# Softmax numerators copied SBUF to SBUF into a float32r buffer and transposed there, in a four-layer forward pass on one core

## The chip, the core and the metric

One core of a Trainium2 chip runs the whole program. The metric is the device time of one execution in microseconds, the median of several runs. Every array is float32. "float32r" is the type that the kernel uses for its fast matrix products: float32 bytes, rounded when an engine writes them.

## The reference, cut to what matters

Two blocks that mix a gated spatial product with grouped-query attention, then a gated-linear-attention layer, then a convolutional feed-forward layer, 1024 tokens of width 1024. The change is in the attention of the first two blocks (`D_B` 512, 8 query heads of 64 features, 2 key/value heads):

```python
def attend(qblk):
    sc = jnp.einsum('bqkgd,bskd->bkgqs', qblk, k).astype(jnp.float32) * scale
    p = jax.nn.softmax(sc, axis=-1).astype(v.dtype)
    return jnp.einsum('bkgqs,bskd->bqkgd', p, v)
```

After it, `x = x + rmsnorm(concat(y_a, y_b) @ w_out) * post_g`, where `y_a` comes from the spatial half.

## The kernel before, in words

Every float32 product runs as three float32r products over an exact split of each factor into a rounded part (hi) and the rest (lo). `split` (L71) makes a pair: ACT or DVE copies to float32r, DVE subtracts.

The order of TensorE's instructions is that of the program text (`manual_schedule`, L79). The orders on DVE, ACT, POOL and SP are made by a planner with its own estimates of time, before the run. All loads and stores but seven go through SP (`load`, L68), which serves its queue in order: an instruction that waits holds what is queued behind it. The planner puts a load into that queue where it expects its buffer to be free.

The attention of a layer goes by 16 groups (g), a group being 128 query tokens and one key/value head, that is 4 heads. A group has 8 units (u). In the unit (g, u):

- `turn(g, u)` (L479) transposes on PE four blocks of 128 x 128 of the softmax numerators P: two heads, two key tiles. The block is the stationary operand and a float32 identity is streamed through it (L490). ACT and DVE then split the result from PSUM into one of 8 buffers PT (`XA`, L491 to 493). The PSUM tile "tr" has two buffers, and a third one is borrowed in part of the first two groups.
- `scores(g + 1)` (L453) does half of one head's scores for the next group; with every second unit a head is complete, DVE takes its row maximum (L467), and ACT writes exp(S - max) as float32 into one of 7 buffers (`XB`, L468 and 470). The heads are made in the order 0, 2, 1, 3. Heads 0 and 2 are transposed in units 0 to 3 of the next group, heads 1 and 3 in units 4 to 7.
- `attend` (L505) multiplies V with the PT of three units before.
- one step of the output projection `project` of an earlier token tile (L533), three products of 512 columns; the first starts at unit 2 of group 2.
- in unit 1 the next queries are transposed, four blocks of 128 x 128 in float32r with the float32r identity `identr` (`prep_turn`, L405); in unit 2 a small gate (L501); in unit 7 of every second group a tile of `y_a` (`turn_ya`, L528, transposes in L147).

In the last group (g = 15), at u = 1, 2, 3, the first three token tiles of the next norm are fetched and normalised in buffers 1, 2, 3 of `XB`, with buffer 3 or 4 as a place for squares that nobody reads (L600 to 602). `XB[:, 7]` holds `qf` and `ya`, the landing places of the queries' and `y_a`'s loads.

Two slots of 32 KiB (`big`, L105) hold the transposed activations h^T in the projections, then PT and P, and at the end the last gate and sums.

Of the kernel before, what the change touches and what calls it, by code (L numbers as in the profile page):

```python
# [36 lines left out]
def build(tc, a):  # L37
    """The whole forward pass on one core.

    Float32 products run as three float32r passes over an exact split x = hi + lo  # L40
    (hi = x rounded to float32r, lo = x - hi): hi*hi + hi*lo + lo*hi.
    """
# [47 lines left out]
    def rstd_of(ss, n=1):  # L90
        """(ss + EPS) ** -0.5"""
        v = T(cst, [128, n], f"ve{n}", bufs=4)
        nc.vector.tensor_scalar(out=v, in0=ss, scalar1=EPS, scalar2=None, op0=ALU.add)  # L93
        r = T(cst, [128, n], f"rs{n}", bufs=4)
        tt(r, v, nhalf[:, 0:n], ALU.pow, nc.gpsimd)
        return r
# [8 lines left out]
    def big(i, dt=F32R):  # L105
        """One of the two 32 KiB slots that hold h^T, the attention's P^T and P, the last gate and sums."""
        return T(xpool, [128, 8192], f"X{i}", dt)

    def hT_half(i):
        return big(i).rearrange("p (s k t) -> p s k t", s=2, k=KT)  # L110

    class Weights:
        """Streams chunks [128, 1024] of packed weights into exact hi/lo pairs, in two pools of 3 and 5 buffers;
        the chunks of the second last for one projection only."""
# [27 lines left out]
    def to_T(src, dst, c0, ps_pool, n, k0=0, tag="tr"):  # L142
        """dst[:, hi/lo, k0 + k, c0:c0 + 128] = src[:, 128 k:128 (k + 1)]^T, k < n."""
        for j in range(0, n, 4):
            ps = T(ps_pool, [128, 4, 128], tag, bufs=2 if tag == "tr" else 1)
            for k in range(4):
                nc.tensor.transpose(ps[:, k], src[:, (j + k) * 128:(j + k + 1) * 128], ident)  # L147
            split(dst[:, 0, k0 + j:k0 + j + 4, c0:c0 + 128],
                  dst[:, 1, k0 + j:k0 + j + 4, c0:c0 + 128], ps, on_act=True)

    def norm_scale(xt, xn, g, junk=None):
        """xn = rmsnorm(xt) * g"""
        ss = T(cst, [128, 1], "ss", bufs=4)
        act(xn if junk is None else junk, xt, AF.Square, scale=1.0 / 32, accum_out=ss)
        r = rstd_of(ss)
        stt(xn, xt, r, g, ALU.mult, ALU.mult)
# [7 lines left out]
    def mm3(ps, L, R, n):  # L164
        """ps = sum over k < n of L(k)^T R(k); L(k, s), R(k, s) give the hi (0) and lo (1) parts."""
        steps3(ps, L, R, range(n), 0, n - 1)

    def stat(hT, t):
        h, c = hT[t // 4], (t % 4) * 128
        return lambda k, s: h[:, s, k, c:c + 128]  # L170
# [9 lines left out]
    class Norms:  # L180
        """The token tiles of one norm, two ahead of their transposes into h^T."""
# [19 lines left out]
        def turn(self, j, tag="tr"):  # L201
            if self.at % 4 == 0 and j == 0:
                self.hT.append(hT_half(self.at // 4))
            t = self.at
            to_T(self.ready[t][:, 512 * j:], self.hT[t // 4], (t % 4) * 128, self.ps, 4, 4 * j, tag)
            self.at += j
# [10 lines left out]
    # ------------------------------------------------------------------ the first two layers  # L217
# [8 lines left out]
    for l in range(2):  # L226
# [11 lines left out]
        # A: norm, projections, gated spatial mixing  # L238
# [107 lines left out]
        def rope(dst, sq, qn, ps, n, i, t):  # L346
            """dst = rope(rmsnorm(ps) * g) of n heads of 64 for token tile t; sq and qn are for its use."""
# [27 lines left out]
        def turn_k(t):  # L375
            """K^T of the two heads, each in both halves of the partitions."""
            kd = kds.pop(t)
            pk = tr(F32R)[:, 0:2]
            for s in range(2):
                nc.tensor.transpose(pk[:, s], kd[:, s], identr)  # L380
            for v in range(2):
                for e in range(2):
                    nc.scalar.copy(Kst[64 * e:64 * e + 64, :, v, t * 128:t * 128 + 128], pk[64 * v:64 * v + 64])
# [27 lines left out]
        def gate_b(u, ps, th):  # L411
            """silu(g_b)^T * 2, a block of 128 features by 512 tokens; 4 steps."""
            hf, j = 1 - u // 4, u % 4
            for k in range(0, KT, 2):
                steps3(ps, wcols(ws[j:j + 1], 128), lambda k, s: hT[hf][:, s, k, :], range(k, k + 2), 0, KT - 1)
                if k < KT - 2:
                    yield
# [13 lines left out]
        # B: attention and, one token tile behind, the output projection  # L431
# [6 lines left out]
        XB = big(1, F32).rearrange("p (u k) -> p u k", u=8)  # L438
        qf, ya = XB[:, 7, 0:512], XB[:, 7, 512:1024]
# [13 lines left out]
        def scores(g):  # L453
            """Group g = (token tile, kv head): S, its maximum, exp; 8 steps."""
# [3 lines left out]
            for hh in (0, 2, 1, 3):  # L458
# [9 lines left out]
                P[hh] = XB[:, count[1] % 7]  # L468
                count[1] += 1
                act(P[hh], ps, AF.Exp, bias=nm, accum_out=sm[:, hh:hh + 1])  # L470
# [8 lines left out]
        def turn(g, u):  # L479
            """P^T of two heads for two key tiles, split; the gate over the row sums first."""  # L480
# [4 lines left out]
            ptr = T(psL, [128, 4, 128], "o" if third else "tr", bufs=1 if third else 2)  # L485
            ptr = ptr.rearrange("p (k e) t -> p k e t", k=2)
            for k in range(2):
                for e in range(2):
                    kt = 2 * k2 + k
                    nc.tensor.transpose(ptr[:, k, e], P[pr + 2 * e][:, kt * 128:kt * 128 + 128], ident)  # L490
            PT = XA[:, count[0] % 8]  # L491
            count[0] += 1
            split(PT[:, 0], PT[:, 1], ptr, on_act=True)
# [39 lines left out]
        def project(qt):  # L533
            """x_new(t) = x(t) + rmsnorm(y(t) w_out) * g_post; 16 steps."""
# [27 lines left out]
        XA = big(0).rearrange("p (u s k h t) -> p u s k h t", u=8, s=2, k=2, h=2)  # L562
# [4 lines left out]
        def step(*ks):  # L567
            """The next step of the oldest projection, if it is one of these, once for each unit (g, u)."""
# [7 lines left out]
        for g in range(2 * NT):  # L576
# [6 lines left out]
            for u in range(8):  # L583
# [15 lines left out]
                if g == 2 * NT - 1 and u in NU:  # L599
                    i = NU.index(u) + 1  # L600
                    norms.fetch(XB[:, i])
                    norms.start(XB[:, i], XB[:, 3 if i < 3 else 4])
# [14 lines left out]
    # ------------------------------------------------------------------ gated linear attention  # L617
# [27 lines left out]
    def f3(ps, L, R, start=True, stop=True):  # L645
        """ps (+)= L^T R of hi/lo pairs."""
# [12 lines left out]
    def split_alpha():  # L659
        """The low-rank weights: pairs of 16 columns [hi lo]; the rows of the second matrix are hi, the bias's hi  # L660
        and lo, hi and lo, against the rows hi, 1, lo and hi of the low-rank activations."""
# [11 lines left out]
    def alpha_low():  # L673
        for hf in range(2):
            ps = gmm()
            for k in range(KT):
                for s in range(2):
                    mm(ps, was[:, k], hT[hf][:, s, k, :], k == 0 and s == 0, k == KT - 1 and s == 1)
# [6 lines left out]
    def decays(h):  # L685
        """With b the running sum of log_sigmoid(...) / 16 over each tile of 128, less its value halfway:
        exp(b), exp(-b) and the decay from the middle of a tile to the middle of the next."""
# [24 lines left out]
    def chunks(h, v, rs, kT, sT, qq, gd):  # L712
        """The chunks of head h and their gated norm; two steps each."""
# [30 lines left out]
    for h in range(4):  # L744
# [4 lines left out]
        def of(x):  # L749
            """The hi and lo parts of tile t of a pair."""  # L750
# [20 lines left out]
        # k and q: feature-major, with their decays  # L771
# [3 lines left out]
        for hf in range(2):  # L775
            ps = gmm().rearrange("p (t i) -> p t i", t=4)
            mm3(ps.rearrange("p t i -> p (t i)"), wcols(ws, 128), lambda k, s: hT[hf][:, s, k, :], KT)
# [21 lines left out]
        for hf in range(2):  # L799
            ps = gmm().rearrange("p (t i) -> p t i", t=4)  # L800
            mm3(ps.rearrange("p t i -> p (t i)"), wcols(ws, 128), lambda k, s: hT[hf][:, s, k, :], KT)
# [11 lines left out]
        # silu(r), token-major, with the scores and, two tiles behind, the chunks  # L813
# [25 lines left out]
    # its output projection, and the next norm  # L839
# [6 lines left out]
    def turn_y(t):  # L846
        """y(t)^T; two steps."""
# [6 lines left out]
    def turn_x(t):  # L854
        """The norm of x_new(t) and its transpose; two steps."""
        xn = T(pH, [128, 1024], "xn", bufs=3)
        norm_scale(xts.pop(t), xn, g_pre)
        for j in (0, 4):
            to_T(xn[:, 128 * j:], hT[t // 4], (t % 4) * 128, psH, 4, j)
# [30 lines left out]
    # ------------------------------------------------------------------ convolutional FFN  # L890
# [12 lines left out]
    def up_mm(ps, w, hf):  # L903
        mm3(ps[:, 512 * hf:512 * hf + 512], w, lambda k, s: hT[hf][:, s, k, :], KT)
# [14 lines left out]
    def gsplit(n):  # L919
        gT = gX[:, n % 4]  # L920
# [4 lines left out]
    for hf in range(2):  # L925
        for n, (w, ps) in enumerate(first):
            up_mm(ps, w, hf)
            if hf == 0 and n == 1:
                to_T(xn, hT[1], 384, psU, KT)
            if hf == 1:  # L930
                up_use(n, ps)
    for n in range(3, 2 * FT):
# [3 lines left out]
        if n == 2 * FT - 1:  # L936
            gX = big(0).rearrange("p (u s k) -> p u s k", u=4, s=2)
# [8 lines left out]
    acc = big(1, F32).rearrange("p (t c) -> p t c", t=NT)  # L946
    load(acc, x_cur.rearrange("(t p) c -> p t c", p=128))
# [13 lines left out]
    def finish(t):  # L961
        """Two steps: the first half of the columns has its gain already."""
        act(acc[:, t, 0:512], acc[:, t, 0:512], AF.Identity, scale=rs[t])
        yield
        stt(acc[:, t, 512:], acc[:, t, 512:], rs[t], gf[:, 512:], ALU.mult, ALU.mult)
        load(tok(a["out"], t), acc[:, t])
        yield

    for c in range(2):
# [18 lines left out]
        for i, t in enumerate(order):  # L988
# [4 lines left out]
            sl = acc[:, t, 512 * c:512 * c + 512]  # L993
# [33 lines left out]
def _cols(w, n):  # L1027
    """[1024 or more rows, c] -> chunks [128, 1024]: for each block of n columns, groups of 1024 // n row tiles."""
# [56 lines left out]
```

## Time and profile before

| | |
|---|---|
| median of 3 runs | 2269.79 us (2268.68 to 2269.9) |
| span of the profiled execution, first to last instruction | 2268.4 us |
| granted TensorE clock, mean | 0.998 |
| busy: PE, DVE, ACT | 99%, 63%, 33% of the span |
| chain of work that ended last | PE 92%, DVE 3%, ACT 2% |
| attention of layer 0, first transposition to the last of its group 15 | 274.3 to about 541.3 us |
| attention of layer 1, the same | 824.1 to about 1091 us |

Of the profiled execution the profile gives the span alone. It lies 1.4 us under the median of the runs; what stands around it is not traced. The profile counts matmuls with their pipeline time, so "PE 99%" says that PE had work nearly always, not that it ran at its peak. What a change is worth is read from starts that follow each other.

### The profile page before, as it was taken

Reading aid. Unit: us, or ns where it says so; the run is one execution under the profiler, and the core shown is the slowest. Engines: PE = TensorE matmul, PEld = TensorE weight load, DVE = VectorE, ACT = ScalarE, POOL = GpSimd, SP = SyncE. Lnnn points to the kernel's source line nnn. Section 1 sums busy time; section 2 is a strip of 40 time slices with the busy share of each in tenths; the row PEclk is TensorE's granted clock in tenths of the full one; section 3 lists DMA queues with packets and bytes.
Section 4 is the critical chain, followed back from the end, with each engine's and each line's share of the span. In section 5 each row is a group of like instructions: output and inputs, shape, how many; then the busy total and the mean of one; then the engine's idle time right before and its main releaser. Section 6 shows DMA issues by size and latency. Waiting matters only on the chain.

```text
span 2268.4 us, 30078 instructions
## 1 busy us (share of the span) xinstructions
PE 2239.4 (99%) x12196; PEld 1923.9 (85%) x12196; DVE 1420.0 (63%) x2169; ACT 747.8 (33%) x1401; POOL 157.3 (7%) x210
## 2 busy tenths in 40 slices
PE   9999999999999999999999999999999999999998
PEld 7888888888788878888899999888888888888887
DVE  7545788888844578888755655645554555554644
ACT  4203276665212146666532322221111111111102
POOL 1004200000101500000100100100000000000000
PEclk9999999999999999999999999999999999999999
DMA  5131401114321231111411112532111111131111
GB/s 191 62 122 38 158 24 58 56 37 145 114 72 65 75 126 43 43 56 63 154 45 59 47 56 78 175 102 76 54 49 47 47 47 56 47 121 47 47 56 75
DMA packets 65036, 171.93 MB, mean 76 GB/s; under 512 B 7680, under 2 KB 20352, under 8 KB 64896
## 3 DMA queue, kind: packets, MB, share of 16 engines
q1 hardware_dynamic: 63888, 166.33, 22.0%
q10 hardware_dynamic: 1008, 3.67, 0.6%
q8 instruction: 96, 1.57, 0.3%
q14 instruction: 44, 0.36, 0.1%
HBM read 136.94 MB, written 33.03 MB: 75 GB/s over the span
## 4 chain that ended last, share of the span: by engine, by line
PE 92%; DVE 3%; ACT 2%; issue 1%; DMA 1%; POOL 0%; POOLq 0%; SPq 0%; ACTq 0%; DVEq 0%
PE mm L63 33%; PE u L63 21%; PE d L63 10%; PE po L63 7%; PE o L63 7%; PE S L63 6%; PE tr L490 4%; PE tr L147 1%; DVE X L57 1%; ACT X L66 1%; DVE nm L467 0%; POOL rs L57 0%; PE big L63 0%; ACT X L73 0%; PE tr L405 0%
## 5 line engine op out<-in xcount | busy, mean ns | idle before, releaser
L63 PE MATMUL mm<-w,X 128*128 128x512 f32 (+1 forms) x3072 | 552.2, 338 | 2.3 <-DVE w L57 1.3
L63 PEld LDWEIGHTS mm<-w,X 128*128 128x128 f32 x3072 | 476.7, 190 | 64.0 <-DVE w L57 2.1
L63 PE MATMUL u<-X,w 128*128 128x512 f32 x2112 | 479.3, 389 | 0.8 <-DVE xt L57 0.8
L63 PEld LDWEIGHTS u<-X,w 128*128 128x128 f32 x2112 | 396.2, 188 | 83.4 <-DVE xt L57 1.2
L57 POOL TENSOR_TENSOR rs<-ve,nhalf 128x1 f32<-128x1 f32 (+2 forms) x136 | 109.8, 808 | 2078.6 <-DVE ve L93 2077.7
L63 PE MATMUL d<-w,X 128*128 128x512 f32 x1056 | 240.0, 389 | 0.2 <-DVE X L57 0.2
L57 DVE TENSOR_TENSOR X<-tr,X 128x512 fp32r<-128x512 f32 x300 | 204.4, 684 | 47.9 <-ACT X L73 44.9
L63 PEld LDWEIGHTS d<-w,X 128*128 128x128 f32 x1056 | 198.0, 188 | 41.9 <-DVE X L57 0.9
L75 DVE CAST w<-raw 128x1024 fp32r<-128x1024 f32 x132 | 93.2, 707 | 214.6 <-PE u L63 192.7
L73 ACT CAST X<-tr 128x512 fp32r<-128x512 f32 x300 | 173.5, 585 | 142.1 <-PE tr L490 77.4
L57 DVE TENSOR_TENSOR w<-raw,w 128x1024 fp32r<-128x1024 f32 x160 | 195.3, 1222 | 3.5 <-ACT w L73 1.0
L63 PE MATMUL S<-K,qT 128*128 128x512 f32 x512 | 178.9, 430 | 2.6 <-DVE t L60 1.4
L467 DVE TENSOR_REDUCE nm<-S 128x1 f32<-128x1024 f32 x128 | 155.9, 1218 | 25.6 <-PE S L63 25.2
L63 PEld LDWEIGHTS po<-X,V 128*128 128x128 f32 x1024 | 151.6, 189 | 22.8 <-DVE ol L57 6.8
L63 PE MATMUL po<-X,V 128*128 128x256 f32 x1024 | 167.7, 287 | 2.0 <-DVE ol L57 1.8
L66 ACT ACTIVATE X<-S,nm 128x1024 f32<-128x1024 f32 x128 | 142.9, 1116 | 62.2 <-DVE nm L467 62.0
L66 ACT ACTIVATE c<-u,cb,cw 128x1024 f32<-128x1024 f32 x44 | 53.2, 1208 | 317.5 <-PE u L63 317.5
L63 PE MATMUL mm<-X,w 128*128 128x512 f32 x672 | 155.5, 390 | 0.0
L490 PE MATMUL tr<-ident,X 128*128 128x128 f32 x960 | 144.7, 273 | 4.7 <-ACT qT L406 2.1
L63 PEld LDWEIGHTS mm<-X,w 128*128 128x128 f32 x672 | 125.3, 188 | 25.5
L490 PEld LDWEIGHTS tr<-ident,X 128*128 128x128 f32 x960 | 110.7, 139 | 12.4 <-DVE X L57 3.9
L60 DVE SCALAR_TENSOR_TENSOR c<-u,cw,c 128x1023 f32<-128x1023 f32 x88 | 112.6, 1280 | 1.5
(207 smaller groups left out, 2302.2 us busy)
## 6 DMA issues: line engine op xcount, KB each, us to landing
raw<-w_in SPq DMA_DIRECT2D x46, 512.0 KB, 3.5
raw<-w_up SPq DMA_DIRECT2D x44, 512.0 KB, 3.3
xt<-x SPq DMA_DIRECT2D x37, 512.0 KB, 3.7
raw<-gla_w_in SPq DMA_DIRECT2D x24, 512.0 KB, 3.6
raw<-w_down SPq DMA_DIRECT2D x22, 512.0 KB, 3.3
raw<-w_out SPq DMA_DIRECT2D x16, 512.0 KB, 3.3
x<-xt SPq DMA_DIRECT2D x16, 512.0 KB, 2.6
y<-yA SPq DMA_DIRECT2D x16, 256.0 KB, 2.0
```

The costliest lines, as they stand in the source:

```text
L57: (eng or nc.vector).tensor_tensor(out=out, in0=in0, in1=in1, op=op)
L60: nc.vector.scalar_tensor_tensor(out=out, in0=in0, scalar=scalar, in1=in1, op0=op0, op1=op1)
L63: nc.tensor.matmul(out, lhsT, rhs, start=start, stop=stop)
L66: nc.scalar.activation(out=out, in_=in_, func=func, **kw)
L73: nc.scalar.copy(hi, src)
L75: nc.vector.tensor_copy(hi, src)
L147: nc.tensor.transpose(ps[:, k], src[:, (j + k) * 128:(j + k + 1) * 128], ident)
L467: nc.vector.reduce_max(out=nm, in_=ps, axis=AX.X, negate=True)
L490: nc.tensor.transpose(ptr[:, k, e], P[pr + 2 * e][:, kt * 128:kt * 128 + 128], ident)
```

## The change

The two slots of 32 KiB become four of 16 KiB (`quarter`); h^T is a list of two quarters for each half of the tokens, and every access to it goes through one more index. In the attention:

- exp writes to one of 3 staging buffers of float32 (`pf`, in `XB`); a DMA issued from SP copies it, 512 KB, into one of 8 buffers of float32r type (`XR`), as plain float32 bytes.
- the four transpositions of a unit read that buffer and stream `identr`; their PSUM tile is float32r, and the split reads it as float32.
- PT has 4 buffers rather than 8.
- `qf` and `ya` move to `XB[:, 3]`. The tiles of the next norm use `XB[:, 0]` to `XB[:, 2]` and, for all three, `XB[:, 3]` for the squares.
- at the end the sums are two tiles, loaded by two DMAs of 2 MB rather than one of 4 MB.

```diff
-    def big(i, dt=F32R):
-        return T(xpool, [128, 8192], f"X{i}", dt)
+    def quarter(i, dt=F32R):
+        return T(xpool, [128, 4096], f"X{i}", dt)
+    def hT_quarter(i):
+        return quarter(i).rearrange("p (s k t) -> p s k t", s=2, k=4)
     def hT_half(i):
-        return big(i).rearrange("p (s k t) -> p s k t", s=2, k=KT)
+        return [hT_quarter(2 * i), hT_quarter(2 * i + 1)]
+    def feat(h):
+        return lambda k, s: h[k // 4][:, s, k % 4, :]
...
-        XB = big(1, F32).rearrange("p (u k) -> p u k", u=8)
-        qf, ya = XB[:, 7, 0:512], XB[:, 7, 512:1024]
+        XB = quarter(2, F32).rearrange("p (u k) -> p u k", u=4)
+        qf, ya = XB[:, 3, 0:512], XB[:, 3, 512:1024]
+        XR = [x[:, j] for x in (quarter(i).rearrange("p (u k) -> p u k", u=4) for i in (3, 1)) for j in range(4)]
...
-                P[hh] = XB[:, count[1] % 7]
+                pf, P[hh] = XB[:, count[1] % 3], XR[count[1] % 8]
                 count[1] += 1
-                act(P[hh], ps, AF.Exp, bias=nm, accum_out=sm[:, hh:hh + 1])
+                act(pf, ps, AF.Exp, bias=nm, accum_out=sm[:, hh:hh + 1])
+                load(P[hh].bitcast(F32), pf)
...
-            ptr = T(psL, [128, 4, 128], "o" if third else "tr", bufs=1 if third else 2)
+            ptr = T(psL, [128, 4, 128], "o" if third else "tr", F32R, bufs=1 if third else 2)
...
-                    nc.tensor.transpose(ptr[:, k, e], P[pr + 2 * e][:, kt * 128:kt * 128 + 128], ident)
-            PT = XA[:, count[0] % 8]
+                    nc.tensor.transpose(ptr[:, k, e], P[pr + 2 * e][:, kt * 128:kt * 128 + 128], identr)
+            PT = XA[:, count[0] % 4]
             count[0] += 1
-            split(PT[:, 0], PT[:, 1], ptr, on_act=True)
+            split(PT[:, 0], PT[:, 1], ptr.bitcast(F32), on_act=True)
...
-        XA = big(0).rearrange("p (u s k h t) -> p u s k h t", u=8, s=2, k=2, h=2)
+        XA = quarter(0).rearrange("p (u s k h t) -> p u s k h t", u=4, s=2, k=2, h=2)
...
                     i = NU.index(u) + 1
-                    norms.fetch(XB[:, i])
-                    norms.start(XB[:, i], XB[:, 3 if i < 3 else 4])
+                    norms.fetch(XB[:, i - 1])
+                    norms.start(XB[:, i - 1], XB[:, 3])
...
-    acc = big(1, F32).rearrange("p (t c) -> p t c", t=NT)
-    load(acc, x_cur.rearrange("(t p) c -> p t c", p=128))
+    accs = [quarter(i, F32).rearrange("p (t c) -> p t c", t=4) for i in (2, 3)]
+    for i, x in enumerate(accs):
+        load(x, x_cur[512 * i:512 * i + 512].rearrange("(t p) c -> p t c", p=128))
+    acc = lambda t, c: accs[t // 4][:, t % 4, c]
```

## Rows read from the trace of the kernel before

**Rows 1.** The page: busy time by engine, and the chain that ended last.

```profile
PE 2239.4 (99%) x12196; PEld 1923.9 (85%) x12196; DVE 1420.0 (63%) x2169; ACT 747.8 (33%) x1401; POOL 157.3 (7%) x210
...
PE 92%; DVE 3%; ACT 2%; issue 1%; DMA 1%; POOL 0%; POOLq 0%; SPq 0%; ACTq 0%; DVEq 0%
```

**Rows 2.** Windows: groups 0 and 1 of layer 0, then four steady groups.

```profile
core 0: us, PE busy (x) PEld busy (x) DVE busy (x) ACT busy (x) POOL busy (x), PEclk, DMA share, GB/s
275.00:300.00 25.00, 22.08 (x151) 18.76 (x150) 23.39 (x37) 18.83 (x36) 0.00 (x0) 1.00 0.24 72
330.00:400.00 70.00, 70.00 (x451) 61.75 (x450) 58.92 (x94) 46.48 (x90) 1.11 (x2) 1.00 0.17 53
```

**Rows 3.** Timeline of PE, units 1 to 4 of group 5: start, length, instruction.

```profile
356.57 0.45 PE L405 MATMUL tr<-identr,qs 128*128 128x128 f32 x4
356.85 0.94 PE L63 MATMUL o<-w,yb 128*128 128x512 f32 x3
357.62 0.64 PE L63 MATMUL po<-X,V 128*128 128x256 f32 x4
358.10 0.60 PE L490 MATMUL tr<-ident,X 128*128 128x128 f32 x4
358.45 0.70 PE L63 MATMUL S<-K,qT 128*128 128x512 f32 x2
359.00 0.38 PE L501 MATMUL tr<-ident,rb 128*128 128x128 f32 x2
...
359.69 0.85 PE L63 MATMUL o<-w,ya 128*128 128x512 f32 x3
360.38 0.60 PE L490 MATMUL tr<-ident,X 128*128 128x128 f32 x4
...
362.45 0.60 PE L490 MATMUL tr<-ident,X 128*128 128x128 f32 x4
```

**Rows 4.** Groups of PE instructions by line and form: busy, mean ns, idle before.

```profile
L490 PE MATMUL tr<-ident,X 128*128 128x128 f32 x960 | 144.7, 273 | 4.7 <-ACT qT L406 2.1 <-DVE X L57 1.2 <-DVE ya L57 1.1
...
L405 PE MATMUL tr<-identr,qs 128*128 128x128 f32 x128 | 14.7, 237 | 0.0
```

**Rows 5.** Timeline: an exp in group 0, one in group 8, their first transpositions.

```profile
283.31 1.12 ACT L66 ACTIVATE X<-S,nm 128x1024 f32<-128x1024 f32 x1
...
287.27 0.60 PE L490 MATMUL tr<-ident,X 128*128 128x128 f32 x4
...
417.45 1.12 ACT L66 ACTIVATE X<-S,nm 128x1024 f32<-128x1024 f32 x1 [0.75 <-DVE nm L467]
...
423.51 0.60 PE L490 MATMUL tr<-ident,X 128*128 128x128 f32 x4
```

**Rows 6.** DMA issues: KB each, median us from issue to landing.

```profile
xt<-x SPq DMA_DIRECT2D x37, 512.0 KB, 3.7
...
x<-xt SPq DMA_DIRECT2D x16, 512.0 KB, 2.6
...
X<-y SPq DMA_DIRECT2D x16, 256.0 KB, 2.7
...
xg<-xt SPq DMA_DIRECT2D x8, 512.0 KB, 5.3
```

**Rows 7.** Timeline of SP's queue in group 8: start and length of issuing.

```profile
413.96 0.32 SPq L69 DMA_DIRECT2D x<-xt  x1
416.57 0.33 SPq L69 DMA_DIRECT2D xt<-x  x1
```

**Rows 8.** Timeline: the end of layer 0's attention (group 15 from 527.9).

```profile
510.72 0.33 SPq L69 DMA_DIRECT2D X<-y  x1
...
528.19 1.11 ACT L66 ACTIVATE X<-S,nm 128x1024 f32<-128x1024 f32 x1
...
535.38 1.06 ACT L66 ACTIVATE X<-X 128x1024 f32<-128x1024 f32 x1
...
541.79 0.60 PE L147 MATMUL tr<-ident,X 128*128 128x128 f32 x4
```

More of the change, by code (lines that the diff above doesn't have):

```diff
@@ L169, in stat @@
         h, c = hT[t // 4], (t % 4) * 128
-        return lambda k, s: h[:, s, k, c:c + 128]
+        return lambda k, s: h[k // 4][:, s, k % 4, c:c + 128]
     def wcols(ws, ncol):
@@ L204, in turn @@
             t = self.at
-            to_T(self.ready[t][:, 512 * j:], self.hT[t // 4], (t % 4) * 128, self.ps, 4, 4 * j, tag)
+            to_T(self.ready[t][:, 512 * j:], self.hT[t // 4][j], (t % 4) * 128, self.ps, 4, 0, tag)
             self.at += j
@@ L414, in gate_b @@
             for k in range(0, KT, 2):
-                steps3(ps, wcols(ws[j:j + 1], 128), lambda k, s: hT[hf][:, s, k, :], range(k, k + 2), 0, KT - 1)
+                steps3(ps, wcols(ws[j:j + 1], 128), feat(hT[hf]), range(k, k + 2), 0, KT - 1)
                 if k < KT - 2:
@@ L677, in alpha_low @@
                 for s in range(2):
-                    mm(ps, was[:, k], hT[hf][:, s, k, :], k == 0 and s == 0, k == KT - 1 and s == 1)
+                    mm(ps, was[:, k], feat(hT[hf])(k, s), k == 0 and s == 0, k == KT - 1 and s == 1)
             sl = aT[:, hf * 512:hf * 512 + 512]
@@ L776, in build @@
             ps = gmm().rearrange("p (t i) -> p t i", t=4)
-            mm3(ps.rearrange("p t i -> p (t i)"), wcols(ws, 128), lambda k, s: hT[hf][:, s, k, :], KT)
+            mm3(ps.rearrange("p t i -> p (t i)"), wcols(ws, 128), feat(hT[hf]), KT)
             ts_ = slice(4 * hf, 4 * hf + 4)
@@ L800, in build @@
             ps = gmm().rearrange("p (t i) -> p t i", t=4)
-            mm3(ps.rearrange("p t i -> p (t i)"), wcols(ws, 128), lambda k, s: hT[hf][:, s, k, :], KT)
+            mm3(ps.rearrange("p t i -> p (t i)"), wcols(ws, 128), feat(hT[hf]), KT)
             ts_ = slice(4 * hf, 4 * hf + 4)
@@ L858, in turn_x @@
         for j in (0, 4):
-            to_T(xn[:, 128 * j:], hT[t // 4], (t % 4) * 128, psH, 4, j)
+            to_T(xn[:, 128 * j:], hT[t // 4][j // 4], (t % 4) * 128, psH, 4)
             yield
@@ L903, in up_mm @@
     def up_mm(ps, w, hf):
-        mm3(ps[:, 512 * hf:512 * hf + 512], w, lambda k, s: hT[hf][:, s, k, :], KT)
+        mm3(ps[:, 512 * hf:512 * hf + 512], w, feat(hT[hf]), KT)
     def up_use(n, ps):
@@ L919, in gsplit @@
     def gsplit(n):
-        gT = gX[:, n % 4]
+        gT = gX[n % 4]
         split(gT[:, 0], gT[:, 1], gs[:, n % FT])
@@ L928, in build @@
             if hf == 0 and n == 1:
-                to_T(xn, hT[1], 384, psU, KT)
+                for j in range(2):
+                    to_T(xn[:, 512 * j:], hT[1][j], 384, psU, 4)
             if hf == 1:
@@ L936, in build @@
         if n == 2 * FT - 1:
-            gX = big(0).rearrange("p (u s k) -> p u s k", u=4, s=2)
+            gX = [x[:, u] for x in (quarter(i).rearrange("p (u s k) -> p u s k", u=2, s=2) for i in (0, 1))
+                  for u in range(2)]
             gTs = [gsplit(k) for k in range(2)]
@@ L961, in finish @@
     def finish(t):
-        act(acc[:, t, 0:512], acc[:, t, 0:512], AF.Identity, scale=rs[t])
+        act(acc(t, slice(0, 512)), acc(t, slice(0, 512)), AF.Identity, scale=rs[t])
         yield
-        stt(acc[:, t, 512:], acc[:, t, 512:], rs[t], gf[:, 512:], ALU.mult, ALU.mult)
-        load(tok(a["out"], t), acc[:, t])
+        stt(acc(t, slice(512, 1024)), acc(t, slice(512, 1024)), rs[t], gf[:, 512:], ALU.mult, ALU.mult)
+        load(tok(a["out"], t), acc(t, slice(0, 1024)))
         yield
@@ L992, in build @@
             next(done, None)
-            sl = acc[:, t, 512 * c:512 * c + 512]
+            sl = acc(t, slice(512 * c, 512 * c + 512))
             tt(sl, sl, ps[t], ALU.add)
```

## The prediction

> **What bounds the kernel now.** I read the page first: PE is busy 99% of the span, DVE 63%, ACT 33%, and 92% of the chain that ended last is PE's [rows 1]. So time goes only where PE's instructions get shorter or PE waits less. The change touches the two attention stages, so I asked for windows of them next. In a steady stretch of 70 us PE shows no idle time at all, DVE is busy 58.92 us (84%), ACT 46.48 us (66%), and the TensorE clock is at its full level, 1.00 [rows 2]. Before that stretch, in groups 0 and 1, where no projection fills the units, it is another picture: DVE is busy 23.39 of 25 us and PE 22.08 [rows 2]. There DVE sets the pace, and a shorter PE instruction is worth nothing. The third view is PE's timeline, read from start to start, because the lengths overlap [rows 3].
>
> **What is removed: the float32 transpositions.** In the steady unit the four float32 transpositions begin at 358.10 and the next product at 358.45: 0.35 us. The two products behind them, 512 columns each, take 0.55 us to the next start (359.00), where 512 columns cost 0.23 each in a plain run (three from 359.69 to 360.38 are 0.69): 0.09 more than 0.46. The four cost PE 0.35 + 0.09 = 0.44 us [rows 3]. The trace before also holds the float32r form, for the queries, with the same identity, tile and neighbours: four from 356.57 to 356.85, 0.28 us, and the three products behind them take 0.77 (to 357.62) rather than 0.69, 0.08 more: 0.36 us [rows 3]. The difference is 0.08 us, each term read to 0.01; I take 0.075 us for a unit of 2.07 us (360.38 to 362.45 [rows 3]).
>
> Of 128 units in a layer the first 16 (groups 0 and 1) go at DVE's pace and give nothing; 112 remain, 224 in both layers: 224 x 0.075 = 16.8 us. If every unit paid and each 0.08, it would be 256 x 0.08 = 20.5 us, the upper bound.
>
> The mean lengths of one, 273 ns in float32 and 237 ns in float32r [rows 4], differ by 36 ns; four would be 0.14 us a unit. I don't use them, since these lengths overlap.
>
> The Trainium skill ("TensorE: Matmul & The Clock Gate", section "Part 4: PE-mode transpose") says that a transposition takes some 275 ns in a kernel, that the latency of PE's access to SBUF dominates it, and that the full clock doesn't engage for it. The length agrees (273 ns [rows 4]); the clock does not, it is 1.00 through the stretch full of them [rows 2]. Taken as a rule for the cost it makes the type irrelevant and the gain nil; that is rival D.
>
> **What is added: 128 copies of 512 KB, SBUF to SBUF.** A copy costs no engine but SP, 0.33 us of issuing each [rows 7], 42 us of a queue that mostly waits. A layer's period is 34.9 us for 8 of them (two groups; 8 x 512 KB / 34.9 us = 120 GB/s), over 53 GB/s at a DMA share of 0.17 [rows 2]: by that ratio the share rises to some 0.55, so the DMA engines have room. No row shows an SBUF-to-SBUF transfer. The nearest of this size land 2.6 us after issue as a store, 3.7 as a load of x, 5.3 for the slowest kind [rows 6]. I take 3.3, between store and load, and keep 2.6 and 5.3. With issuing that is 3.6 us from the end of exp.
>
> What hides it is the time from the end of exp to the first transposition of that head. I went through all 128 heads. The median is 7.1 us. Of the steady ones the shortest recurs in every odd group, head 2: exp ends at 417.45 + 1.12 = 418.57 and is needed at 423.51, 4.94 us [rows 5]; units that are 0.075 shorter take 5 x 0.075 = 0.38 from it, 4.56 remain. 3.6 fits. The shortest of all is head 2 of group 1: 283.31 + 1.12 = 284.43, needed at 287.27, 2.84 us (2.95 to the block that reads it, the second) [rows 5]. There the copy is 0.7 us late. That is 0.7 us a layer, 1.4 in all, on PE's path (0 at 2.6, and 2.7 a layer at 5.3).
>
> The copy also makes SP wait for exp, and what is queued behind it waits too: the store of x and the load of the next x (413.96 and 416.57 [rows 7]), the loads of queries, gates and `y_a`. They are wanted one token tile later, some 30 us, so I cost them at nothing. The other way round, a copy queued behind that pair waits for it: see rival B. I add 0.5 us for odd collisions.
>
> **What moves at the end of each attention.** Before, the load of `y_a` for the last tile went out at 510.72, long before its use at 541.79 [rows 8]. Now `ya` lies in `XB[:, 3]`, into which all three norm tiles write their squares; the load must wait for the last of these. And the first norm tile is fetched to `XB[:, 0]`, the staging buffer of the very last head (63 mod 3 = 0), whose exp ends at 528.19 + 1.11 = 529.30 [rows 8]. The chain: copy 3.6 us to 532.9, fetch 0.33 + 3.7 to 536.9, square 1.06 and its read-out to 538.2, then the load of `ya`, 0.33 + 2.7 [rows 6], to 541.2, if the other two squares are done by then. PE wants it at 541.79, less the last group's 8 x 0.075: 541.2. If the planner keeps the order 0, 1, 2, the two other tiles come behind, 1.3 us of ACT each: about 2.6 us late. I take 1 us a layer, 2 in all, bounds 0 and 2.6.
>
> **What I cost at nothing.** PT in 4 buffers: the unit that writes a buffer follows in PE's order the product that read it, and the split waits for that unit's transpositions anyway. The cover is the lag of three units; with a lag of 4, each unit would wait. P in 8 buffers rather than 7: a head's buffer was emptied a group earlier. The quarters of h^T: same instructions, same order on PE. Two loads of 2 MB in place of one of 4: they land during the first half of the last products.
>
> **What takes some of it back.** The PSUM tile "tr" has two buffers; a unit waits until DVE has taken the unit before last. In the rows of the transpositions PE idled 4.7 us in all for such things [rows 4]. A faster PE meets them more often, as DVE's 84% becomes 58.92 / (70 x 1.99 / 2.07) = 88%. I take 1.5 us, bounds 0 and, if DVE's order eats most of the gain, 12 (rival C).
>
> Sum: -16.8 + 1.4 + 0.5 + 2 + 1.5 = -11.4 us. Against the span that is 2268.4 - 11.4 = 2257.0; the median of the runs is 1.4 us over the span, so 2258.4. I predict 2258.5.
>
> **The rivals.**
>
> B, slower: SP's order makes the copies late. In every second group the queue holds the store of x and the load that waits for it to land, 416.57 - 413.96 = 2.61 us apart [rows 7]. If the planner puts head 2's copy behind that pair, it starts up to 2.9 us later: 2.9 + 3.6 = 6.5 us against the 4.56 that remain, 2 us of waiting a token tile; with a landing of 5.3 us it is 4 us. 7 tiles, two layers: 28 to 56 us, so 2286 to 2314, I name 2290. For it: the order is fixed from estimates, before the run. Against: the load goes out at 416.57 and exp ends at 418.57, so in today's order the copy comes after the pair. It decides from 4.56 us between exp and landing; the gain of some 11 us is gone at 5.4.
>
> C, no difference: DVE and ACT become the bound. If their fixed orders allow the unit to shrink by 0.025 rather than 0.075, the gain is 224 x 0.025 = 5.6 against some 3.9 of late copies: 2268. For it: DVE was the bound in groups 0 and 1 at 94% [rows 2]. Against: DVE would be at 88%, and the waits are few.
>
> D, the type doesn't matter: no gain, the late copies stay: 2269.8 + 4 = 2274. Against it stand the float32r rows between the same neighbours [rows 3].
>
> E, more: no late copies, the ring doesn't bind, 0.08 a unit: 224 x 0.08 = 18, so 2252.
>
> **How the numbers follow.** What a measurement of this kernel can tell from no change is about 0.2%, 4.5 us. My forecast has 0.57, E 0.13, C 0.13, B 0.13, D 0.04. Faster by over 0.2% (below 2265.3): forecast and E, 0.70. Within: C and most of D, 0.17. Slower: B, 0.13. The range takes in E, the forecast's own bounds (slowest landing in the first groups, 2.7 x 2, and the late `ya`, 2.6 x 2: +7) and C: 2250 to 2271. B and D are left out.
>
> **What would show it.** In the profile after: L490's float32r transpositions with 0.28 to the next start, and units of 1.99 us in the steady groups; 128 copies landing in 2.6 to 3.7 us; PE idle before L490 with a copy as its releaser only in groups 1 and 2; at the end of each attention a wait of PE in front of the transpositions of `ya` with a load as its releaser; the second attention as much shorter as the first. A steady unit of 2.07 would mean D, or C if PE idles; a wait for a copy in each odd group would mean B. A landing above 4.5 us would make the forecast wrong at once.

## The result, and the profile after

The changed kernel takes 2282.38 us (median of 4 runs, 2280.62 to 2284.19) where the kernel before takes 2269.23 in the same comparison: a ratio of 1.0063, 95% interval 1.0049 to 1.0078. The forecast was 2258.5, range 2250 to 2271, with 0.13 for slower: it was wrong in sign. The profiled execution took 2280.62 us, its span is 2278.8, 10.4 more than before.

What the change was made of came as forecast; what went wrong lies beside it. First the page of after, busy time and chain, which answers to [rows 1]:

```profile
PE 2232.1 (98%) x12196; PEld 1910.5 (84%) x12196; DVE 1418.2 (62%) x2169; ACT 748.0 (33%) x1401; POOL 156.6 (7%) x210
...
PE 90%; DVE 3%; issue 2%; ACT 1%; DMA 1%; POOL 1%; POOLq 0%; ACTq 0%; DVEq 0%; SPq 0%
```

PE is busy 7 us less in a span that is 10 us longer: it waits. The windows that answer to [rows 2] show that it waits in the steady groups, where it had not been idle at all (2 of 70 us), and that the traffic of the copies is there, 173 GB/s for 53. The 0.93 in the first window is one stretch, 295.6 to 299.0 us, at a granted clock of 0.50, after PE had worked only 1.82 of the 3.6 us before it:

```profile
core 0: us, PE busy (x) PEld busy (x) DVE busy (x) ACT busy (x) POOL busy (x), PEclk, DMA share, GB/s
275.00:300.00 25.00, 21.10 (x142) 17.90 (x141) 22.30 (x35) 17.61 (x34) 0.00 (x0) 0.93 0.58 216
330.00:400.00 70.00, 68.04 (x446) 58.94 (x445) 58.20 (x94) 45.85 (x88) 1.11 (x2) 1.00 0.46 173
```

PE's timeline, units of group 5, answers to [rows 3] (start, length, instruction). Four transpositions to the next product take 0.30 us (0.35 before), the two products behind them 0.53 (0.55), and the unit from 361.27 to 363.26 takes 1.99 (2.07):

```profile
359.05 0.46 PE L499 MATMUL tr<-identr,X 128*128 128x128 f32 x4
359.35 0.70 PE L63 MATMUL S<-K,qT 128*128 128x512 f32 x2
359.88 0.38 PE L510 MATMUL tr<-ident,rb 128*128 128x128 f32 x2
...
361.27 0.46 PE L499 MATMUL tr<-identr,X 128*128 128x128 f32 x4
...
363.26 0.46 PE L499 MATMUL tr<-identr,X 128*128 128x128 f32 x4
```

The groups by form answer to [rows 4]: the mean fell from 273 to 240 ns, but PE's idle time ahead of these instructions rose from 4.7 to 17.9 us. The issues by kind answer to [rows 6]: a copy lands in 2.9 us.

```profile
L499 PE MATMUL tr<-identr,X 128*128 128x128 f32 x960 | 112.9, 240 | 17.9 <-issue 8.2 <-DVE ve L93 5.0 <-ACT qT L413 2.4
```

```profile
X<-X SPq DMA_DIRECT2D x128, 512.0 KB, 2.9
```

**First place: the ends of the groups.** The last unit of every odd group takes 3.28 us rather than 2.50, unit 3 of every even group 2.70 rather than 2.30 (medians over groups 2 to 13 of both layers, from PE's timeline, first transposition to first transposition). All other units are shorter. At the end of group 5, PE and DVE of after:

```profile
369.26 0.46 PE L499 MATMUL tr<-identr,X 128*128 128x128 f32 x4
...
370.79 0.60 PE L154 MATMUL tr<-ident,X 128*128 128x128 f32 x4
...
372.54 0.51 PE L499 MATMUL tr<-identr,X 128*128 128x128 f32 x4 [0.68 <-issue]
```

```profile
370.28 1.22 DVE L475 TENSOR_REDUCE nm<-S 128x1 f32<-128x1024 f32 x1
371.43 0.41 DVE L57 TENSOR_TENSOR gb<-ol,gb 64x256 f32<-64x256 f32 x1
371.76 0.68 DVE L57 TENSOR_TENSOR X<-tr,X 128x512 fp32r<-128x512 f32 x1
```

And DVE, then PE, of before, the same place:

```profile
369.70 0.42 DVE L57 TENSOR_TENSOR gb<-ol,gb 64x256 f32<-64x256 f32 x1
370.04 0.68 DVE L57 TENSOR_TENSOR X<-tr,X 128x512 fp32r<-128x512 f32 x1
370.64 1.21 DVE L467 TENSOR_REDUCE nm<-S 128x1 f32<-128x1024 f32 x1
```

```profile
368.65 0.60 PE L490 MATMUL tr<-ident,X 128*128 128x128 f32 x4
...
371.15 0.60 PE L490 MATMUL tr<-ident,X 128*128 128x128 f32 x4
```

Of the two "tr" buffers one is taken by the unit at 369.26, the other by `ya` at 370.79. The next transpositions need the first back, and it comes back when DVE's subtract (`X<-tr,X`) has read it. Before, that subtract went ahead of the row maximum (`nm<-S`, 1.22 us) and ended at 370.72, 0.43 us before PE needed the buffer at 371.15; after, the maximum goes first, the subtract ends at 372.44, and PE starts at 372.54. Same instructions, another order. The row names "issue" as the releaser, not DVE; that it was the subtract is read from the two timelines, and e2, e3 and e9 bear it out.

The even groups have the same with another pair: the gate's product goes ahead of `ve`, the first step of a norm's root, which POOL and the 1.28 us of `xt` follow, and `ol` behind them is what PE's `po` waits for (DVE, then PE, of after):

```profile
342.93 0.42 DVE L60 SCALAR_TENSOR_TENSOR gb<-gb,tr 128x256 f32<-128x256 f32 x1
343.26 0.15 DVE L93 TENSOR_SCALAR ve<-ss 128x1 f32<-128x1 f32 x1
344.08 1.28 DVE L60 SCALAR_TENSOR_TENSOR xt<-tmp,rs,xt 128x1024 f32<-128x1024 f32 x1 [0.67 <-POOL rs L57]
345.39 0.43 DVE L57 TENSOR_TENSOR ol<-po,ol 64x256 f32<-64x256 f32 x1
```

```profile
345.88 0.74 PE L63 MATMUL po<-X,V 128*128 128x256 f32 x4 [0.30 <-DVE ol L57]
```

Before, `ve` went first:

```profile
341.91 0.15 DVE L93 TENSOR_SCALAR ve<-ss 128x1 f32<-128x1 f32 x1
341.99 0.42 DVE L60 SCALAR_TENSOR_TENSOR gb<-gb,tr 128x256 f32<-128x256 f32 x1
```

**Second place: the end of each attention.** The chain that ended last, from 531 us on:

```profile
531.83 4.30 DMA X<-X
...
536.14 4.29 DMA X<-x
...
543.99 1.06 ACT X L66 x2
545.05 0.02 issue
545.07 2.73 DMA X<-y
547.79 0.14 issue
547.93 1.09 PE tr L154 x4
```

The last head's copy, the fetch of a norm's tile into the buffer that it was copied from, its squares, the load of `ya` over them, PE. The windows show what it costs (columns as above), two of after, then one of before:

```profile
541.00:544.70 3.70, 1.25 (x10) 0.97 (x8) 2.34 (x5) 3.67 (x8) 0.65 (x2) 1.00 0.01 2
544.70:551.50 6.80, 5.36 (x24) 4.57 (x23) 4.93 (x8) 1.52 (x4) 1.00 (x2) 0.50 0.51 195
```

```profile
541.00:551.50 10.50, 10.50 (x67) 9.10 (x66) 7.97 (x15) 7.01 (x13) 0.55 (x1) 1.00 0.02 7
```

PE works 1.25 of 3.7 us, and for the next 6.8 the granted clock is 0.50, the 1.2 GHz level (in layer 1 the same, 1097.7 to 1104.5 us); before, neither: PE works through all of that stretch. Two of PE's waits of that end in after, with what was waited for, total, times and longest:

```profile
PE tr L499 <- DVE ve L93: 2.4, 1, 2.4
...
PE tr L154 <- DMA X<-y: 1.4, 1, 1.4
```

### The profile page after: what moved, and what is told of

Same layout as the page of the kernel before. It is cut to its first block, busy times and chain, and to the rows that moved or that the text cites. A ratio compares the mean times of both kernels' runs of the same rounds, so it can differ in the third digit from the quotient of the medians.

```text
span 2278.8 us, 30544 instructions
## 1 busy us (share of the span) xinstructions
PE 2232.1 (98%) x12196; PEld 1910.5 (84%) x12196; DVE 1418.2 (62%) x2169; ACT 748.0 (33%) x1401; POOL 156.6 (7%) x210
## 4 chain that ended last, share of the span: by engine, by line
PE 90%; DVE 3%; issue 2%; ACT 1%; DMA 1%; POOL 1%; POOLq 0%; ACTq 0%; DVEq 0%; SPq 0%
PE mm L63 33%; PE u L63 21%; PE d L63 10%; PE po L63 8%; PE S L63 6%; PE o L63 6%; PE tr L499 3%; PE tr L154 1%; ACT X L66 1%; POOL rs L57 1%; DVE xt L60 1%; PE tr L412 0%; PE big L63 0%; DMA X<-x 0%; PE tr L63 0%
## 5 line engine op out<-in xcount | busy, mean ns | idle before, releaser
L499 PE MATMUL tr<-identr,X 128*128 128x128 f32 x960 | 112.9, 240 | 17.9 <-issue 8.2
L499 PEld LDWEIGHTS tr<-identr,X 128*128 128x128 f32 x960 | 100.4, 140 | 28.5 <-issue 10.3
```

## The experiments

Two theories stood at the start: the float32r transpositions led the planner to another order on DVE and that order costs the time; or the copies cost it. Both turned out to hold a part. This table gives for each kernel the median, the ratio to before in the same comparison with its interval, and three stretches of the profiled execution, read from PE's timeline: groups 0 to 14 of both layers together; the end of layer 0, from the start of its group 15 to the first transposition of layer 1's attention; and the end of layer 1, from its group 15 to the last instruction.

| kernel | median us | ratio (95%) | groups 0-14 | end 0 | end 1 |
|---|---|---|---|---|---|
| before | 2269.23 | | 507.2 | 296.2 | 1190.8 |
| after | 2282.38 | 1.0063 (1.0049, 1.0078) | 510.9 | 297.9 | 1196.0 |
| e1 float32, copies | 2280.39 | 1.0056 (1.0041, 1.0071) | 507.9 | 302.3 | 1196.6 |
| e2 float32r, no copies | 2269.57 | 1.0006 (0.9997, 1.0016) | 510.8 | 292.1 | 1189.5 |
| e3 order | 2267.07 | 0.9993 (0.9983, 1.0002) | 497.9 | 299.7 | 1193.8 |
| e4 squares | 2282.14 | 1.0063 (1.0047, 1.0079) | 510.8 | 298.3 | 1195.6 |
| e5 order, fetch | 2260.54 | 0.9960 (0.9948, 0.9973) | 497.6 | 295.9 | 1191.1 |
| e6 fetch | 2272.63 | 1.0020 (1.0011, 1.0029) | 510.9 | 294.4 | 1191.9 |
| e7 buffers | 2268.90 | 1.0000 (0.9991, 1.0009) | 508.6 | 292.0 | 1189.9 |
| e8 maximum only, fetch | 2261.54 | 0.9971 (0.9959, 0.9983) | 499.6 | 293.7 | 1190.2 |
| e9 before, maximum first | 2282.50 | 1.0060 (1.0046, 1.0074) | 520.1 | 297.5 | 1190.4 |
| e10 order, no copies | 2255.82 | 0.9944 (0.9931, 0.9958) | 497.2 | 291.9 | 1189.9 |
| e11 order, fetch by POOL | 2259.85 | 0.9960 (0.9947, 0.9974) | 497.5 | 293.3 | 1191.1 |

**e1: the copies with float32 transpositions.**

```diff
...
-nc.tensor.transpose(ptr[:, k, e], P[pr + 2 * e][:, kt * 128:kt * 128 + 128], identr)
+nc.tensor.transpose(ptr[:, k, e], P[pr + 2 * e].bitcast(F32)[:, kt * 128:kt * 128 + 128], ident)
...
```

> The changed kernel with the copies and the quarter buffers kept, but the numerators transposed in float32 again (the changed kernel's transposes against the float32 identity). VectorE's order of the steady part is then that of the kernel before. Theory 1 (the float32r transposes led the planner to another order on VectorE, and that order holds TensorE up; the copies cost nothing): the regular stalls of +0.84 us at the odd groups' ends and +0.47 us in the middle of the even groups are gone, the unit is 2.07 us again, and only the late load of ya at the end of each attention is left, 2.5 us a layer, with the clock stretch behind it: 2269 + 5 to 10 = 2274 to 2279 us. Theory 2 (the copies hold up TensorE or its buffers): the stalls stay and the gain of the transposes, 16 us, is lost as well: about 2298 us.

2280.4 us, between the two. The groups are those of before to 0.01 us (17.40 us an even group, 17.54 an odd one): the copies don't hold them up, and the order of before is back with the type. But both ends lost 6 us each, and PE's waits name the load of `ya`, with 4.2 us a layer rather than the 2.5 expected:

```profile
PE tr L154 <- DMA X<-y: 8.3, 2, 4.2
```

So the order was not all: with it undone, the copies cost 11 us at the ends.

**e2: float32r without the copies.**

```diff
-act(pf, ps, AF.Exp, bias=nm, accum_out=sm[:, hh:hh + 1])
-load(P[hh].bitcast(F32), pf)
+act(P[hh], ps, AF.Exp, bias=nm, accum_out=sm[:, hh:hh + 1])
```

> The changed kernel without the copies: the exponential writes the float32r buffer itself, so the numerators are rounded to float32r (it leaves out their low parts), and the transposes stay float32r. VectorE's order is that of the changed kernel. Theory 1 (order): 2282 us as changed, within 3, with the same two stalls of 0.84 and 0.47 us; up to 2 less where a copy landed late. Theory 2 (copies): the stalls are gone and the unit of 2.00 us shows: about 2262 us or less.

2269.6 us; neither theory's figure. The groups keep both stalls (3.32 us for the odd groups' last unit, 2.70 for the even groups' unit 3), so these come with the type, not with the copies. PE's waits of this kernel name DVE where after says "issue":

```profile
PE tr L498 <- DVE X L57: 8.7, 12, 0.7
PE po L63 <- DVE ol L57: 5.7, 14, 0.7
```

The ends gained, 5.8 and 6.5 us on after. The 13 us between after and e2 lie at the ends.

**e3: the order put back.**

```diff
...
-nc.vector.reduce_max(out=nm, in_=ps, axis=AX.X, negate=True)
+with tc.issue_after(last_lo[0]) if hh in (3,) and last_lo[0] is not None else ExitStack():
+    nc.vector.reduce_max(out=nm, in_=ps, axis=AX.X, negate=True)
...
-stt(gr, gr, 0.5, pr_, ALU.mult, ALU.mult)
+with tc.issue_after(ve_ins[0]) if kv == 0 and 2 <= qt else ExitStack():
+    stt(gr, gr, 0.5, pr_, ALU.mult, ALU.mult)
```

> The changed kernel with VectorE's order put back by hand: the row maximum of the fourth head queued behind the low-part subtract of a group's last unit, and the gate's product behind the first instruction of the norm's root. Nothing else differs. Theory 1 (order): per layer 7 stalls of 0.84 us and 6 of 0.47 us go, 8.7 us: 2282.4 - 17.4 = 2265 us. Theory 2 (copies): 2282 us, the stalls stay. Rival to both (the stall moves, since VectorE is nearly full: 2.0 us a unit leaves it less room): between 2268 and 2280 us, with new waits of TensorE for VectorE elsewhere.

2267.1 us, 15.3 less than after. The stalls are gone (2.43 and 2.36 us), an even group takes 17.03 us, an odd one 17.01, and groups 0 to 14 lose 13.0 us against after. Of these, 1.9 us lie in group 1 of layer 0 (16.08 us in after, 14.21 here), where the half-clock stretch of after is gone. The ends are still late: PE waits 7.7 us for `X<-y`.

**e4: the squares to another buffer.**

```diff
-norms.start(XB[:, i - 1], XB[:, 3])
+norms.start(XB[:, i - 1], XR[i - 1])
```

> The changed kernel with one address changed: the squares that the first three norms of the next stage throw away go to a float32r buffer of a finished group instead of the buffer that ya shares. Theory (the load of the last ya waits for the third of these squares and for the row that it is taken from): the wait for ya, 2.5 us a layer, goes, and with it the half-clock stretches at 544.7 and 1097.7 us, 6.8 us long and so worth up to 3.4 us each: 2282.4 - 5 - (0 to 7) = 2270 to 2277 us. If the load waits for something else, 2282 us.

Nothing: 2282.1 us. The load of `ya` went out at 512.82 us rather than 545.07, and PE's wait only changed its name: in after it was 5.0 us of the unit's transpositions for `ve` and 3.0 us of `ya` for `X<-y`, in both layers together, and here it is this one:

```profile
PE tr L499 <- DVE X L57: 7.6, 2, 3.8
```

Two pieces of the chain that ended last, then DVE:

```profile
531.92 3.71 DMA X<-X
...
535.70 3.12 DMA X<-x
```

```profile
540.02 0.15 DVE L93 TENSOR_SCALAR ve<-ss 128x1 f32<-128x1 f32 x1 [1.33 <-ACT X L66]
540.90 1.28 DVE L60 SCALAR_TENSOR_TENSOR X<-X,rs,gpre 128x1024 f32<-128x1024 f32 x1 [0.73 <-POOL rs L57]
...
544.57 0.67 DVE L57 TENSOR_TENSOR X<-tr,X 128x512 fp32r<-128x512 f32 x1
```

The fetch of the norm's tile waits for the landing of the last copy, because it goes to the buffer that the copy reads. DVE serves its queue in order and stands at the norm's root; the split that PE waits for is behind it. So it is the fetch, not the place of `ya`, that has to move.

**e5: order and fetch.** To e3's edit comes:

```diff
-norms.fetch(XB[:, i - 1])
-norms.start(XB[:, i - 1], XB[:, 3])
+if i == 1:
+    XN = quarter(3, F32).rearrange("p (u k) -> p u k", u=4)
+norms.fetch(XN[:, i])
+norms.start(XN[:, i], XN[:, 0])
```

> The changed kernel with VectorE's order put back by hand (as in e3) and the first three token tiles of the next norm fetched into the quarter that the numerators of the last group but one have left, rather than into the three buffers that the exponentials write and the last copies read. Theory (two separate causes: the order of VectorE in the steady part, and the late fetch of these tiles at the end of each attention): both gone, 2267.1 less 8.4 us at each attention's end (between the attentions 280.0 us as without the copies against 288.4 in e3): 2250 us, within 2247 to 2256, with no TensorE wait on a DMA at the end of the attention. Rival (the end waits for ya or for VectorE wherever the tiles lie): 2264 to 2268 us.

2260.5 us, 0.4% faster than before, and no wait for a DMA at the end of the attention; but 6.5 us less than e3, not 17. I had compared e3's 288.4 us between the attentions with the 280.0 of e2, where the exponentials leave the fetch's buffers alone from the start. Part of the rest may be one half-clock stretch in the projections of layer 1 (576.1 to 579.5 us at 0.51), which before has as well at 581.9.

**e6: the fetch alone.** e5's second edit on the changed kernel.

> The changed kernel with the fetch moved as in e5, VectorE's order left as changed. Theory (the copies themselves cost TensorE nothing; that e2 without them was 13 us faster came from the three buffers that the last copies hold): as e2, 2270 us, within 2267 to 2273. Rival (the copies cost by their traffic or by SP's queue): 2277 to 2283 us.

2272.6 us, 9.8 less than after and 3.1 more than e2, without copies: within what was expected, at its upper end. Groups 0 to 14 are after's.

**e7: the buffers alone.** The quarters, with float32 transpositions and no copies.

> Only the quarter buffers of the change: the exponentials write the numerators once, there are no copies, and the transposes are float32. VectorE's order is that of the kernel before. Theory: the buffers alone cost nothing; at the ends of the attentions they rather give what e2 showed, 280.0 against 283.4 us between the attentions: 2262 to 2269 us. Against e1 (the same with the copies, 2280.4) the difference, 11 to 18 us, is what the copies cost by the late fetch alone. If the buffers by themselves hold up the end: 2275 to 2281 us.

2268.9 us, no difference to before. Against e1, which is this with the copies, 11.5 us.

**e8: one swap of two.** e5 without the second `issue_after` of e3.

> As e5, but only the row maximum is put back behind the subtract; the gate's product stays ahead of the norm's root. If the two swaps cost what their stalls were in the trace of the changed kernel (7 of 0.84 us at the odd groups' ends from the maximum, 6 of 0.35 to 0.47 us in the even groups from the gate, a layer): e5 plus 4 to 6 us, 2254 to 2257 us. If the maximum alone held both up: e5 within 1 us.

The odd groups keep 17.01 us, the even ones go from 17.03 to 17.37, so the two swaps are separate, as expected; but groups 0 to 14 take only 2.0 us more than e5, where 4 to 6 were expected. The medians, 2261.5 and 2260.5, don't resolve it.

**e9: the same order forced on the kernel before.** The subtract of unit 7 is put behind the maximum; nothing of the change is in.

```diff
...
+with tc.issue_after(last_max[0]) if kv == 1 else ExitStack():
+    tt(pt_[:, 1], ps_, pt_[:, 0], ALU.subtract)
```

> The kernel before, with one thing of the change's order forced on it: the low-part subtract of each group's last unit is queued behind the row maximum of the fourth head. Buffers, transposes and numerators are those of before, and there are no copies. Theory (VectorE's order costs this by itself, whatever the type of the transposes): the last unit of the odd groups grows from 2.50 us by 0.5 to 0.84 us, 7 times a layer, the even groups stay: 2268.7 + 7 to 12 = 2276 to 2281 us. Rival (the order hurts only together with the faster transposes or the copies): within 2 of 2268.7 us.

2282.5 us, above the range expected: this one swap makes the kernel before as slow as the changed one. The odd groups' last unit takes 3.35 us rather than 2.50, an odd group 18.58 rather than 17.54: 0.85 us in that unit, and the rest mostly in unit 1 (2.62 for 2.43). The second swap was not forced on the kernel before; e8 has it alone. DVE and PE of this kernel:

```profile
371.29 1.21 DVE L469 TENSOR_REDUCE nm<-S 128x1 f32<-128x1024 f32 x1
372.43 0.67 DVE L57 TENSOR_TENSOR X<-tr,X 128x512 fp32r<-128x512 f32 x1
```

```profile
373.25 0.63 PE L492 MATMUL tr<-ident,X 128*128 128x128 f32 x4 [0.69 <-DVE X L57]
```

**e10: order, no copies.**

> The order put back as in e3, without the copies (the exponential writes float32r itself; it leaves out the numerators' low parts), the fetch as in the changed kernel. It bounds what the copies still cost in e5. Theory (they cost nothing where the fetch doesn't wait for them): as e5, 2260.5 us, within 2254 to 2262; the steady groups 17.01 us as in e5. If the copies hold up the steady groups by traffic or landing: groups under 16.9 us and 2250 us or less.

2255.8 us, and 17.01 us a group as in e5, with 128 copies fewer. In the steady groups the copies cost nothing that shows; what they cost, 4.7 us against e5 and 4.0 against e11, lies at the ends; what holds PE up there, no run takes apart. Against e2, which has no copies either, this kernel undoes the order alone: groups 0 to 14 lose 13.6 us, about as many as with copies (13.0).

**e11: the fetch from POOL's queue.** `nc.gpsimd` issues the three fetches; the rest is e5.

> As e5, but the three fetches at the end of the attention are issued from GpSimd's queue, so that they don't stand behind the copies in SyncE's. In e5 they were issued at 521.7 to 525.9 us though their buffer was free some 15 us before. Theory (what e5 still lost in the last group, 0.6 to 1.05 us where the other odd groups gained 0.5, is the late fetch): 2260.5 - 2 to 3 = 2257 to 2259 us. If it is the order of VectorE's work there: 2260 to 2261 us. If GpSimd's issue holds up the norm's roots that it computes: 2262 to 2266 us.

2259.9 us, not told apart from e5. The expectation had a wrong premise: the quarter was not free 15 us before. POOL, too, could issue only at 521.31, when PE had transposed the last of group 14:

```profile
521.31 1.83 POOL L198 DMA_DIRECT2D X<-x  x3 [9.41 <-PE tr L503]
```

## Why the prediction was wrong, by its own steps

The sum had -11.4 us, the spans say +10.4: 21.8 apart. The failed step is the term for the ring of "tr" and DVE's order, taken at 1.5 us and measured at 13.0; the end of each attention, taken at 2 us in all, is second, with 7.6. Groups 0 to 14 of after against e3 give 13.0 of it, the ends of after against e6 give 3.5 + 4.1 = 7.6, of which 2 were in the sum, and the gain itself was 2.9 short: without the swaps (e3) groups 0 to 14 lie 9.3 us below before, where the sum had, for the 208 units of groups 2 to 14, 208 x 0.075 - 1.4 - 0.5 - 1.5 = 12.2. That makes 21.5.

- **What takes some of it back: the step that failed.** I took 1.5 us for the ring of "tr" and DVE's order, bounds 0 and 12, by asking how full DVE would be in the order that it had. The planner made a new order, and the two swaps cost 13.0 us (e3; 13.6 without copies, e10 against e2), beyond the upper bound. That orders are made from estimates I had held against SP (rival B); for DVE I reckoned with the order that stood (rival C), where a ring of two with three users at an odd group's end left 0.43 us of slack, not 1.2. e9 shows that the order of the maximum does this alone. In 1.5 us of group 1 of layer 0 the copies have a part: with the order of after and copies the clock fell there (after, e4, e6: 16.1 us), without copies it did not (e2: 13.85); how, no run shows. That the order changed with the type of the transpositions is shown by e1 and e2; that it did so because the planner reckons float32r faster is likely, but argued only.
- **The end of each attention.** The chain had the right pieces: copy, fetch, squares, load. I put 1 us a layer on it, bounds 0 and 2.6, as the wait of `ya` alone. Two pieces were too short: the copy took 4.30 us for 3.3, and from the fetch's landing (540.43) to the end of the squares (545.05) it was 4.6 us for 1.3. What was missed is that DVE's queue stands at the norm's root meanwhile (PE waits 2.4 us in layer 0, and 1.4 more for `ya`), and that PE then runs 6.8 us at half clock. e4 shows that the late fetch costs the same with `ya` out of its way.
- **The float32r transpositions.** Taken 0.075 us a unit; a plain unit went from 2.07 to 2.00, and an odd and an even group lost 0.53 and 0.39 us in e5, 0.058 a unit on the mean, since a few units (unit 3 of the even groups, parts of groups 2 and 14) end with a wait for DVE or ACT. Right in kind, 0.017 a unit too large.
- **Rival D** fell: the mean of one is 240 ns for 273 and the unit is shorter. The rule of the Trainium skill ("TensorE: Matmul & The Clock Gate", section "Part 4: PE-mode transpose") that access latency dominates a transposition and the full clock doesn't engage would have made the type irrelevant; the trace of after has 1.00 in the steady window, where products stand between the transpositions, and the type worth 0.07 us a unit, so for this mixture the measurement decides against it. Transpositions by themselves no run shows.
- **The copies.** 2.9 us to land where 3.3 were taken; PE stood 0.5 us in all, twice, before these transpositions for a copy, at the start of group 15 in each layer; taken were 1.4, in group 1, where only weight loads waited, 0.15 and 0.18 us. Rival B, late copies by SP's order, did not come: e10 and e5 have the same steady groups.
- **What I cost at nothing.** The quarters and the four PT buffers cost nothing (e7).
- **Rival C** named the right engine and the right reason, DVE's order, and stopped at a gain eaten up, which is no change. The slower side was given to the wrong queue (rival B).

The gap that repeats at each odd group's end looks like too few buffers, and the Trainium skill ("Perfetto Trace Analysis", section "Optimization Strategy") says of such repeating gaps that there may not be enough PSUM for the next tile. Here the count stayed at two in e3, and the gap went with the order of two DVE instructions: the buffer is short only because its reader comes late.

## What to carry to other kernels

Where a planner orders an engine by estimates, a change of an instruction's type or time on one engine can reorder another, so the first comparison of two traces is the order of each engine's instructions, not their durations. On a buffer ring without slack, ask who frees the buffer and which long instruction could slip ahead of it. And an asynchronous copy extends the life of its source to its landing: whatever reuses that source, here a fetch for the next stage, belongs in the sum.

## What the runs showed of the hardware that was not expected

Copies within SBUF of 512 KB landed in 2.9 us, beside other work of PE that they did not slow (17.01 us a group with and without). They slow other transfers a little: the loads of the queries (`X<-q`, 256 KB) landed in 3.1 us (median, e5) with copies and in 2.7 without (e10). The six fetches at the ends landed in 4.9 us with copies (e5) and in 4.4 without (e10):

```profile
X<-x SPq DMA_DIRECT2D x6, 512.0 KB, 4.9
```

```profile
X<-x SPq DMA_DIRECT2D x6, 512.0 KB, 4.4
```

So most of what they take beyond the 3.7 us of other loads of this size [rows 6] is not the copies' doing. The longest copy seen, in e1, was issued 1.7 us behind the first of two fetches and landed in 6.85:

```profile
529.73 6.85 DMA X<-X
```

A 1.2 us swap of two instructions on an engine that is busy 84% of the time there [rows 2] moved the whole program by 0.6% (e9).
